# RWKV recurrence in phases: TensorE's order written out between small phases and dense units

## The chip, the core and the metric

The kernel runs on one core of a Trainium2 chip. The metric is the time of one execution in device microseconds; times of several executions are told as a median. TensorE (PE in the rows) does matmuls, and its weight loads are a row of their own (PEld); VectorE is DVE, ScalarE ACT, GpSimd POOL, and SyncE (SP) issues the DMAs. Each engine takes its instructions in the order that was fixed when the kernel was compiled; semaphores between engines make an instruction wait for its operands and buffers.

## The reference

One inference step of a two-layer trunk for 512 prompt tokens and 8 samples of 4 tokens, 1024 features. Layer 0 is a SwiGLU, RWKV-7 time mixing and a second SwiGLU; layer 1 has mLSTM in place of RWKV. All in float32. The change is in layer 0, whose core is the recurrence over tokens, with 16 heads of 64 and a state S (64 x 64) for each head:

```python
def step(S, inp):
    r_t, d_t, k_t, v_t, kk_t, b_t = inp
    sa = jnp.einsum('bhvk,bhk->bhv', S, -kk_t)
    S = S * d_t[:, :, None, :] + sa[..., None] * b_t[:, :, None, :] + v_t[..., None] * k_t[:, :, None, :]
    return S, jnp.einsum('bhvk,bhk->bhv', S, r_t)
```

Ahead of it stand the mixes of neighbouring tokens, the projections r, k, v and the low-rank projections of decay, a and gate; behind it a group norm per head, a bonus term, the gate and the output projection.

## The kernel before

**Dense work.** Weights are streamed from HBM in blocks of 128 x 1024 float32 and split into a high and a low part by ScalarE and VectorE (`weight`, `split`, L352 and L353); `mm3` (L356 to L358) then does three matmuls for each 128 x 128 tile. The tokens are worked on in two parts: part 0 is prompt tokens 0 to 255 (256 columns), part 1 prompt tokens 256 to 511 and the 32 sample tokens (288 columns). A unit of dense work is a closure: 24 matmuls for a projection, 48 for one block of the SwiGLU's gate and up projections, 12 to 24 for a block of its down projection.

**The recurrence** is done in chunks of 64 tokens, four heads (two pairs) at a time: m = 0 to 3 for part 0, m = 4 to 7 for part 1. For each m there are
- `rwkv_prep`, for each pair: the low-rank product of decay and a, exponentials, scan and scaled keys; tile `swa` and PSUM bank `pq` have one buffer each;
- `rwkv_quad`: Gram products (L937), masks (L940), rounding (L949, L951), the products `e` on GpSimd (L955), and then the inverse of a triangular matrix by doubling, in rounds between TensorE and ScalarE or VectorE (L959 to L993);
- `rwkv_tokens`: values transposed, bonus;
- `rwkv_chunk`, four times (c = 0 to 3): three rounds between TensorE and VectorE, which carry the state;
- `rwkv_sample` for part 1, for each pair: the samples' own recurrence. It loads the state into `s0` (one buffer, L1076), multiplies it (L1104), and at the end adds the last product (L1135) to it (L1136) and stores it (L1137);
- `rwkv_finish`: norm, gate and split of the pair's output.

`rwkv_slots` goes through 32 slots, t = 4 m + c. In each it writes the chunk, at c = 0 also the quad and values of m + 1, at c = 2 the preparation of m + 2, and at c = 3 the finishes. All of it stands under `high_priority(OFF)`, which puts it ahead of dense work wherever it can run; the scheduler of the compiler, which plays the program through with its own costs, then fixes the order of each engine. After each slot an equal share of the dense units `todo` is written. Slots 0 to 9 have the rest of the first SwiGLU of part 1 and then norm, mixes and the r and k projections of part 1 (`rwkv_first(1)`), slots 10 to 15 its k, gate and v projections, slots 17 to 31 the output projection of part 0 (`rwkv_out(0)`) and its second SwiGLU; `rwkv_out(1)` follows.

Of the kernel before, what the change touches and what calls it, by code (L numbers as in the profile page):

```python
# [28 lines left out]
OFF = 20000  # L29
NMX = 19  # L30
# [218 lines left out]

class Trunk:  # L250
    def __init__(self, tc, nc, a, o, pool):
        self.tc, self.nc, self.a, self.o, self.pool = tc, nc, a, o, pool
        self.n = 0
        self.last = None
        self.hn = {}
        self.V, self.S, self.G, self.T = nc.vector, nc.scalar, nc.gpsimd, nc.tensor

# [203 lines left out]
    def ffn_units(self, name, g, i, groups=(0, 8, 15, FT)):  # L461
# [18 lines left out]
        def up(m):  # L480
            pg, pu = self.bank("pd", 2), self.bank("pd", 2)
            for ps, n in ((pg, "_g"), (pu, "_u")):
                wt = self.weight(self.a[name + n][m])
                for k in range(KT):
                    c = slice(k * P, (k + 1) * P)
                    self.mm3(ps[:, :w_], *wt(c), xs[k][0], xs[k][1], k == 0, k == KT - 1)
            s, w, e = self.t1(w_), self.t1(w_), self.t1(w_)
            V.tensor_tensor(s, pg[:, :w_], rs, op=ALU.mult)  # L488
            V.tensor_tensor(w, pu[:, :w_], rs, op=ALU.mult)
            self.sigmoid(e, s)  # L490
            G.tensor_tensor(s, s, w, op=ALU.mult)
            G.tensor_tensor(s, s, e, op=ALU.mult)
            h[m] = [self.hm(w_) for _ in range(2)]
            self.split(*h[m], s)

        def down(m, k0, k1):
            wt = self.weight(self.a[name + "_d"][m][:, k0 * P:k1 * P])
            ps = self.bank("pd", 2)
            for k in range(k0, k1):
                c = slice((k - k0) * P, (k - k0 + 1) * P)  # L500
                self.mm3(ps[:, :w_], *wt(c), h[k][0], h[k][1], k == k0, k == k1 - 1)
            V.scalar_tensor_tensor(self.x[m][:, hs], ps[:, :w_], 0.5, self.x[m][:, hs], op0=ALU.mult, op1=ALU.add)
        us = [start]
        for k0, k1 in zip(groups, groups[1:]):
            us += [lambda m=m: up(m) for m in range(k0, k1)]
            us += [lambda m=m, k0=k0, k1=k1: down(m, k0, k1) for m in range(KT)]
# [50 lines left out]
    def rwkv(self, before=None, after=None):  # L557


        with self.scope("rw", nps=1):  # L560
# [4 lines left out]
            with self.tc.tile_pool(name="spill", bufs=1, space=DRAM) as dp:  # L565
# [3 lines left out]
                self.d, self.quad, self.st = {}, {}, {}  # L569
                self.chain, self.chain_y = [self.bank("pc", 2) for _ in range(2)]  # L570
                self.nhm = {"mx": NMX, "hm": 8}
                with self.scope("rw1", nps=0):
# [7 lines left out]
                    with self.tc.high_priority(OFF):  # L580
                        self.rwkv_ahead(0)
                        self.rwkv_square(0)
# [3 lines left out]
                    with self.tc.high_priority(OFF):  # L586
                        self.rwkv_value(0)
                        self.rwkv_ahead(1)
# [6 lines left out]
                with self.scope("rw2", nps=0):  # L595
                    with self.tc.high_priority(OFF):
                        self.rwkv_value(ND)
# [101 lines left out]
    def part_dense(self, w, ps, xs, mw=P, first=True, last=True):  # L699
        for k in range(KT):  # L700
            c = slice(k * mw, (k + 1) * mw)
            self.mm3(ps, *w(c), xs[k][0], xs[k][1], first and k == 0, last and k == KT - 1)

    def rwkv_project(self, n, c, i):
# [12 lines left out]
        return [lambda: xs.extend(self.rwkv_mix(c, i))] + [lambda m=m: unit(m) for m in range(KT)]  # L717

    def rwkv_low_rank(self, i):
# [36 lines left out]
        for c, ns in ((1, (("r_w1", P, slice(0, 64), self.hwa),)), (4, (("r_a1", P, slice(64, P), self.hwa),)),  # L756
                      (5, (("r_g1a", P, slice(0, P), self.hg), ("r_g1b", P, slice(0, 96), None)))):
            us.append(lambda c=c: mix(c))
# [3 lines left out]
    def rwkv_first(self, i):  # L762

        low, k = self.rwkv_low_rank(i), self.rwkv_project("k", 2, i)
        return ([lambda: self.rwkv_norm(i)] + low[:4] + self.rwkv_project("r", 0, i) + k[:5],
# [26 lines left out]
    def rwkv_ahead(self, m):  # L792

        if m < 2 * ND:
            self.d[m] = [self.rwkv_prep(2 * (m % ND) + a, m // ND) for a in range(2)]

    def rwkv_square(self, m):
        if m < 2 * ND:
            self.quad[m] = self.rwkv_quad(self.d[m])

    def rwkv_value(self, m):
        if m < 2 * ND:
            uv = self.rp("uv", 2, [P, 1024]).rearrange("p (a c h v) -> p a c h v", a=2, c=4, h=2)
            for a in range(2):
                self.rwkv_tokens(2 * (m % ND) + a, m // ND, self.d[m][a]["v"], uv[:, a])
            self.quad[m] += (uv,)
# [43 lines left out]
    def rwkv_prep(self, j, i):  # L850
        nc, V, S, G, T = self.nc, self.V, self.S, self.G, self.T
# [10 lines left out]
        for e, rows in enumerate(R):  # L862
            ps = self.bank("pq", 1)[:, :w]
# [12 lines left out]
        S.activation(q, k, AF.Square, scale=self.vec("kk", j))  # L876
        ps = self.bank("pq", 1)[:, :w]
# [29 lines left out]
        return {"xc": xc, "xs": xs, "arc": arc, "ars": ars, "pc": pc, "y": k, "v": v}  # L907

    def rwkv_quad(self, ds):
# [3 lines left out]
        V, S, G, T = self.V, self.S, self.G, self.T  # L913
# [16 lines left out]
        xt = self.rp("xt", 2, [P, 1024])  # L930
# [10 lines left out]

        for a, d in enumerate(ds):
            px = self.bank("pq", 1)
            for i in range(4):
                T.transpose(px[:, i * P:(i + 1) * P], flat(d["xc"][:, i]), self.ident)
            S.copy(xt[:, a * 512:(a + 1) * 512], px)
# [10 lines left out]
        e = part(0)  # L957
        pt = pb()
# [5 lines left out]
        for l in range(1, 6):  # L964
            e = part(l)
            p1 = pb()
            each(lambda r, a, b: T.matmul(p1[r, a], e[r, a], ti[r, a], start=True, stop=True))
            p1s = h16("p1s")
            S.copy(p1s, p1[:, :W])
            pd = pb()  # L970
# [7 lines left out]
        pt = pb()  # L978
        each(lambda r, a, b: T.matmul(pt[r, a], ti[r, a], id16[r], start=True, stop=True))
        S.copy(tt, pt[:, :W])  # L980
        pr = pb()

# [4 lines left out]
        each(residual)  # L987
        r_ = self.rp("e", 2, [P, W], F16)
        V.tensor_tensor(r_, pr[:, :W], ti, op=ALU.subtract)
        pf = pb()  # L990
# [3 lines left out]
        return gm, tf, xt  # L994
# [5 lines left out]
    def rwkv_tokens(self, j, i, v, uv):  # L1000

        V, S, T = self.V, self.S, self.T
        R = (slice(0, 64), slice(64, 128))
        r, k = self.r[i][j], self.k[i][j]
        pv = self.bank("pq", 1)
# [6 lines left out]
        V.scalar_tensor_tensor(r, r, self.vec("rk", j), k, op0=ALU.mult, op1=ALU.mult)  # L1012
        ps = self.bank("pq", 1)[:, :r.shape[-1]]
# [3 lines left out]
    def rwkv_chunk(self, m, c):  # L1017

        V, S, T = self.V, self.S, self.T
        R = (slice(0, 64), slice(64, 128))  # L1020
        gm, tf, xt, uv = self.quad[m]
# [10 lines left out]
        pr, pu, pn = reg(c % 2), reg(2), reg(3)  # L1032
        for a in range(2):
# [5 lines left out]
        V.tensor_copy(rhs, pr)  # L1039
        for a in range(2):  # L1040
# [4 lines left out]
        S.copy(uv[R[0], :, c, 1, :], two(pu[R[0]]))  # L1045
        for a, h in pairs:
            z = (a * 4 + c) * P + h * 64
            T.matmul(pn[R[h], col(a)], xt[:, z:z + 64], uv[:, a, c, h, :], start=True, stop=True)
        sn = self.rp("stp", ND, [P, P]) if m < ND and c == 3 else self.rp("sm", 3, [P, P])
        for a in range(2):  # L1050
            if st is None:
                V.tensor_scalar(sn[:, col(a)], pn[:, col(a)], pc[a], None, op0=ALU.mult)
            else:
                V.scalar_tensor_tensor(sn[:, col(a)], pn[:, col(a)], pc[a], sp[:, col(a)], op0=ALU.mult, op1=ALU.add)
        out = lambda a: slice(a * 4 * CH + c * CH, a * 4 * CH + (c + 1) * CH)
        py = self.chain_y
        for a in range(2):
            for h in range(2):
                T.matmul(py[R[h], out(a)], uv[:, a, c, h, :], gm[:, a, c, 1 - h, 64:128], start=True, stop=st is None)  # L1059
            for h in range(2 if st is not None else 0):  # L1060
                T.matmul(py[R[h], out(a)], st[R[h], col(a)], arc[a][R[h], c, 1, :], start=False, stop=True)
        if c == 3:
# [4 lines left out]
    def rwkv_sample(self, j, d):  # L1067
# [3 lines left out]
        H = slice(0, 64)  # L1071
        xs, ars, y, v, pl = d["xs"], d["ars"], d["y"], d["v"], d["pc"][:, 4:]
# [5 lines left out]
        gm = t5().rearrange("p (h t) -> p h t", h=2)  # L1078
        for h in range(2):
            pg = self.ps()  # L1080
            T.matmul(pg[H, :64], xs[R[h]].rearrange("p x t -> p (x t)"),
                     ars[R[h]].rearrange("p x t -> p (x t)"), start=True, stop=True)
            V.tensor_tensor(gm[H, 1 - h, :], pg[H, :64], self.masks[H], op=ALU.mult)
# [4 lines left out]
                        pl.unsqueeze(1).unsqueeze(3).to_broadcast([P, 2, NB, NS]), op=ALU.mult)  # L1088
        px = self.ps()
        T.transpose(px[H, :P], xs.rearrange("p x t -> p (x t)"), self.ident)  # L1090
        xt = t5()
        S.copy(xt[H], px[H, :P])
        vd = nt[:, 64:128]
        G.tensor_copy(vd.rearrange("p (x t) -> p x t", x=2), v[:, HA:].unsqueeze(1).to_broadcast([P, 2, TS]))
        pv = self.ps()
        T.transpose(pv[H, :P], vd, self.ident)
        uv = t5().rearrange("p (h v) -> p h v", h=2)
        for h in range(2):
            S.copy(uv[Q[h], h, :], pv[Q[h], h * 64:(h + 1) * 64])

        pa = self.ps()
        for b in range(NB):
            for h in range(2):
                T.matmul(pa[R[h], b * 8:(b + 1) * 8], s0v[R[h], b, :],  # L1104
                         ars[R[h], :, b * NS:(b + 1) * NS], start=True, stop=True)
        a0 = t5()
# [491 lines left out]
```

## Time and profile before

| | us |
|---|---|
| median of 3 runs | 2540.12 (2539.03 to 2542.99) |
| profiled execution | 2541.78 |
| its span, first to last instruction | 2539.8 |

| engine | busy us in the span | share |
|---|---|---|
| TensorE matmuls | 2445.1 | 96% |
| TensorE weight loads | 2310.1 | 91% |
| VectorE | 1587.1 | 62% |
| ScalarE | 1250.3 | 49% |
| GpSimd | 501.6 | 20% |

Busy times are sums of instruction times. Matmuls are pipelined, and the ends of the records are modelled, so the distance from start to start tells more than a matmul's own time. Idle time counts gaps longer than 0.15 us. The granted clock is a mean over a stretch, 1.0 being the full 2.4 GHz.

### The profile page before, as it was taken

How to read it: one execution, taken by the hardware profiler on the slowest of the kernel's cores; microseconds unless marked ns; L12 is line 12 of the kernel's file. 1: busy time of each engine (PE TensorE's matmuls, PEld its weight loads, DVE VectorE, ACT ScalarE, POOL GpSimd, SP SyncE). 2: the span in 40 equal slices, each digit the busy share in tenths (PEclk: the TensorE clock that was granted, in tenths of full speed). 3: DMA queues.
4: the chain of work that ended last, by engine and by line, in shares of the span. 5: the costliest groups of instructions: out<-in, count | busy, mean ns of one | idle time of the engine just before them, and what ended most of it. 6: DMA issues, size and time to landing. Idle time of an engine off the chain costs nothing.

```text
span 2539.8 us, 54086 instructions
## 1 busy us (share of the span) xinstructions
PE 2445.1 (96%) x21731; PEld 2310.1 (91%) x21731; DVE 1587.1 (62%) x3154; ACT 1250.3 (49%) x2716; POOL 501.6 (20%) x522
## 2 busy tenths in 40 slices
PE   9998999999889999999999999999999999999997
PEld 8998988888778788897899999999978899999997
DVE  6667787787887886765666544443346856444433
ACT  6555666655575564554555433332245545333322
POOL 1203333333432342322011011110000000111100
PEclk9998999999799899999999999999999999999999
DMA  6664543333233223444455522222223322222222
GB/s 215 183 197 130 166 131 120 105 96 120 90 120 103 75 93 113 129 150 146 128 167 164 153 89 90 84 85 88 83 87 112 101 73 92 86 92 90 88 84 73
DMA packets 102218, 291.62 MB, mean 115 GB/s; under 512 B 12568, under 2 KB 28344, under 8 KB 101968
## 3 DMA queue, kind: packets, MB, share of 16 engines
q1 hardware_dynamic: 101968, 288.18, 36.9%
q8 instruction: 170, 2.79, 0.4%
q14 instruction: 80, 0.66, 0.1%
HBM read 278.76 MB, written 9.38 MB: 113 GB/s over the span
## 4 chain that ended last, share of the span: by engine, by line
PE 84%; DVE 9%; issue 2%; ACT 2%; DMA 1%; POOL 1%; SPq 0%; DVEq 0%; ACTq 0%; POOLq 0%
PE ps L356 17%; PE ps L358 17%; PE ps L357 17%; PE pd L356 7%; PE pd L357 7%; PE pd L358 7%; DVE wl L353 2%; DVE m L693 1%; PE ps L1254 1%; PE ps L1256 1%; PE ps L1255 1%; PE b L937 1%; PE ps L1135 1%; DVE mx L695 1%; PE pc L1059 1%
## 5 line engine op out<-in xcount | busy, mean ns | idle before, releaser
L353 DVE TENSOR_TENSOR wl<-wr,wh 128x512 fp32r<-128x512 f32 (+2 forms) x1025 | 723.2, 708 | 479.6 <-ACT wh L352 452.8
L352 ACT CAST wh<-wr 128x512 fp32r<-128x512 f32 (+2 forms) x1025 | 621.8, 609 | 676.6 <-PE ps L357 430.8
L356 PE MATMUL ps<-a,wh 128*128 128x288 f32 (+1 forms) x2384 | 698.0, 293 | 13.5 <-ACT a L404 5.0
L358 PE MATMUL ps<-a,wl 128*128 128x288 f32 (+1 forms) x2384 | 692.6, 291 | 0.0
L357 PE MATMUL ps<-a,wh 128*128 128x288 f32 (+1 forms) x2384 | 686.6, 288 | 0.3
L356 PEld LDWEIGHTS ps<-a,wh 128*128 128x128 f32 x2384 | 452.8, 190 | 16.9 <-DVE raw L1350 5.4
L357 PEld LDWEIGHTS ps<-a,wh 128*128 128x128 f32 x2384 | 452.6, 190 | 1.5 <-DVE a L405 0.8
L358 PEld LDWEIGHTS ps<-a,wl 128*128 128x128 f32 x2384 | 450.0, 189 | 0.5 <-DVE wl L353 0.2
L428 POOL TENSOR_TENSOR t<-t,t 128x256 f32<-128x256 f32 (+1 forms) x132 | 141.7, 1073 | 846.7 <-ACT wh L352 410.1
L356 PE MATMUL ps<-h,wh 128*128 128x288 f32 (+1 forms) x1056 | 303.9, 288 | 0.0
L357 PE MATMUL ps<-h,wh 128*128 128x288 f32 (+1 forms) x1056 | 303.4, 287 | 0.0
L358 PE MATMUL ps<-h,wl 128*128 128x288 f32 (+1 forms) x1056 | 303.2, 287 | 0.0
L356 PE MATMUL pd<-rk,wh 128*128 128x288 f32 (+1 forms) x656 | 199.0, 304 | 6.8 <-DVE t L488 2.9
L358 PEld LDWEIGHTS ps<-h,wl 128*128 128x128 f32 x1056 | 198.9, 188 | 0.0
L357 PEld LDWEIGHTS ps<-h,wh 128*128 128x128 f32 x1056 | 198.9, 188 | 0.0
L357 PE MATMUL pd<-rk,wh 128*128 128x288 f32 (+1 forms) x656 | 198.6, 303 | 0.2 <-DVE gm L679 0.2
L356 PEld LDWEIGHTS ps<-h,wh 128*128 128x128 f32 x1056 | 198.6, 188 | 0.0
L358 PE MATMUL pd<-rk,wl 128*128 128x288 f32 (+1 forms) x656 | 197.2, 301 | 0.0
L352 ACT CAST h<-t 128x256 fp32r<-128x256 f32 (+1 forms) x132 | 55.3, 419 | 198.9 <-POOL t L428 198.9
L357 PE MATMUL pd<-mx,wh 128*128 128x256 f32 (+1 forms) x448 | 135.3, 303 | 9.4 <-DVE mx L695 6.6
L356 PE MATMUL pd<-mx,wh 128*128 128x256 f32 (+1 forms) x448 | 133.8, 302 | 4.3 <-ACT rk L716 1.9
L356 PEld LDWEIGHTS pd<-rk,wh 128*128 128x128 f32 x656 | 128.0, 195 | 10.5 <-ACT mx L694 2.9
(460 smaller groups left out, 4548.4 us busy)
## 6 DMA issues: line engine op xcount, KB each, us to landing
wr<-in_f0a_u_dram SPq DMA_DIRECT2D x44, 512.0 KB, 3.6
wr<-in_f0b_g_dram SPq DMA_DIRECT2D x44, 512.0 KB, 3.6
wr<-in_f0b_u_dram SPq DMA_DIRECT2D x44, 512.0 KB, 3.5
wr<-in_f0a_g_dram SPq DMA_DIRECT2D x43, 512.0 KB, 3.6
wr<-in_f0b_d_dram SPq DMA_DIRECT2D x24, 512.0 KB, 3.6
wr<-in_f1a_g_dram SPq DMA_DIRECT2D x22, 512.0 KB, 4.6
wr<-in_f1a_u_dram SPq DMA_DIRECT2D x22, 512.0 KB, 3.5
wr<-in_f1b_g_dram SPq DMA_DIRECT2D x22, 512.0 KB, 3.5
```

The lines of the kernel that those rows point to most:

```text
L352: self.S.copy(dst_h, src)
L353: self.V.tensor_tensor(dst_l, src, dst_h, op=ALU.subtract)
L356: self.T.matmul(out, wh, xh, start=start, stop=False)
L357: self.T.matmul(out, wh, xl, start=False, stop=False)
L358: self.T.matmul(out, wl, xh, start=False, stop=stop)
L428: self.G.tensor_tensor(s, s, w, op=ALU.mult)
L693: V.scalar_tensor_tensor(m, d, self.vec("mu", c * 8 + k), xn, op0=ALU.mult, op1=ALU.add)
L695: (self.G if k % 2 else V).tensor_tensor(l, m, h.bitcast(F32), op=ALU.subtract)
L937: T.matmul(pg[:, (1 - h) * 512 + i * P:(1 - h) * 512 + (i + 1) * P], flat(xc[R[h], i]), flat(arc[R[h], i]), start=True, stop=True)
L1059: T.matmul(py[R[h], out(a)], uv[:, a, c, h, :], gm[:, a, c, 1 - h, 64:128], start=True, stop=st is None)
L1135: T.matmul(pn[R[h], :], xt[H, h * 64:(h + 1) * 64], um, start=True, stop=True)
L1254: T.matmul(pss[q][:n, :], xs[k][0][:, ts], wt(cs)[0], start=k == 0, stop=False)
```

## The change

The small work is turned into generators: each function yields "s", "pq" or "ps" ahead of each of its TensorE steps. A slot has `SPS` = 4 steps. A step advances each generator that waits at "s" by one step, then writes a share of the dense work, then advances at most one generator waiting at "pq" and one at "ps" (those that need the single banks of these names), and writes another share. Dense units give their number of matmuls as cost, the SwiGLU's gate and up projections are two units instead of one, and the shares follow cost. `ordered` ties each matmul of a phase, and the first and last of each `mm3`, to the one before, and the matmuls of the phases lose the high priority; the other engines' instructions keep it.

The quad's transposes of the chunk's keys are a generator of their own (`rwkv_rows`). The quad's last transpose goes into the second half of the residual's bank. A chunk's new state is written behind its output products. In the sample's recurrence the state product comes first, two transposes share a bank, and some tiles move from bank `ps` to `pq`; `s0` still has one buffer.

```diff
+class Plain:
+    def put(self, f, a, k):
+        with self.t.tc.high_priority(-self.t.off):
+            return self.t.ordered(f(*a, **k))
...
     def mm3(self, out, wh, wl, xh, xl, start, stop):
-        self.T.matmul(out, wh, xh, start=start, stop=False)
-        self.T.matmul(out, wh, xl, start=False, stop=False)
-        self.T.matmul(out, wl, xh, start=False, stop=stop)
+        T = self.PT if self.off else self.T
+        first = T.matmul(out, wh, xh, start=start, stop=False)
+        T.matmul(out, wh, xl, start=False, stop=False)
+        last = T.matmul(out, wl, xh, start=False, stop=stop)
+        if not self.off and self.in_order:
+            if self.order is not None:
+                self.after(first, self.order)
+            self.order = last
...
+    def ordered(self, r):
+
+        if self.in_order:
+            if self.order is not None:
+                self.after(r, self.order)
+            self.order = r
+        return r
...
+    def rwkv_phase(self, places):
+
+        with self.tc.high_priority(OFF):
+            self.off = OFF
+            seen = set()
+            for name in list(self.gens):
+                place = self.gens[name][1]
+                if place in places and (place == "s" or place not in seen):
+                    seen.add(place)
+                    self.advance(name)
+            self.off = 0
...
+        def dense():
+            nonlocal done, k
+            k += 1
+            while todo and done + todo[0][0] / 2 <= total * k / n:
+                c, f = todo.pop(0)
+                done += c
+                f()
         for t in range(t0, t1):
             m, c = divmod(t, 4)
             i, j = divmod(m, ND)
             with self.tc.high_priority(OFF):
+                self.off = OFF
                 if c == 0:
-                    self.rwkv_square(m + 1)
-
-                    if m + 1 != ND:
-                        self.rwkv_value(m + 1)
+                    self.drain("quad", "px", "value", "ahead", "sample")
+                    if m + 1 < 2 * ND:
+                        self.begin("px", self.rwkv_rows(m + 1))
+                        self.begin("quad", self.rwkv_square(m + 1))
+
+                        if m + 1 != ND:
+                            self.begin("value", self.rwkv_value(m + 1))
+                    if i:
+                        self.begin("sample", self.rwkv_samples(m))
                 if c == 2:
-                    self.rwkv_ahead(m + 2)
-                if i and c in (0, 1):
-                    self.rwkv_sample(2 * j + c, self.d[m][c])
-                self.rwkv_chunk(m, c)
+                    self.begin("ahead", self.rwkv_ahead(m + 2))
+                self.begin("chunk", self.rwkv_chunk(m, c))
+                self.off = 0
+            for q in range(SPS):
+                self.rwkv_phase(("s",))
+                dense()
+                self.rwkv_phase(("pq", "ps"))
+                dense()
+            with self.tc.high_priority(OFF):
+                self.off = OFF
+                self.drain("chunk")
                 if c == 3:
-                    for a in range(2):
-                        self.rwkv_finish(2 * j + a, i, m)
-            self.step(-(-len(self.todo) // (t1 - t)))
+                    self.drain("finish", "sample")
+                    self.begin("finish", self.rwkv_finishes(m))
+                if t == 4 * ND or t == 8 * ND - 1:
+                    self.drain("finish")
+                self.off = 0
...
+        yield "s"
         pr = pb()
+        each(lambda r, a, b: T.matmul(pr[r, b], ti[r, a], id16[r], start=True, stop=True))
...
         each(residual)
+        S.copy(tt, pr[:, W:])
...
         pn = self.ps()
         for h in range(2):
+            yield "s"
             um = self.local("um", 1, [64, 512])
```

## Rows read from the trace of the kernel before

**Rows 1.** Busy time by stretch: stretch, length, engines (instructions), granted clock, DMA share, GB/s.

```profile
core 0: us, PE busy (x) PEld busy (x) DVE busy (x) ACT busy (x) POOL busy (x), PEclk, DMA share, GB/s
404.00:640.00 236.00, 230.87 (x2936) 207.37 (x2935) 185.62 (x380) 145.09 (x338) 75.95 (x73) 0.99 0.37 111
640.00:800.00 160.00, 137.39 (x1136) 122.55 (x1137) 136.38 (x272) 103.12 (x258) 57.28 (x75) 0.86 0.30 93
800.00:1090.00 290.00, 280.19 (x3588) 239.62 (x3587) 211.95 (x450) 157.86 (x377) 97.55 (x98) 0.96 0.34 105
1090.00:1195.00 105.00, 104.83 (x896) 95.37 (x896) 67.13 (x141) 55.95 (x120) 28.94 (x31) 1.00 0.54 164
1195.00:1237.00 42.00, 33.11 (x186) 27.28 (x184) 23.22 (x47) 20.64 (x43) 1.03 (x1) 0.84 0.28 88
```

**Rows 2.** Timeline of TensorE, small groups among dense matmuls: start, duration, line, tiles.

```profile
457.35 0.29 PE L358 MATMUL pd<-hm,wl 128*128 128x288 f32 x1
457.58 0.44 PE L971 MATMUL b<-p1s,ti 64*64 64x64 f16 x16
...
459.13 0.40 PE L356 MATMUL pd<-hm,wh 128*128 128x288 f32 x1
459.37 0.29 PE L357 MATMUL pd<-hm,wh 128*128 128x288 f32 x1
459.50 0.30 PE L358 MATMUL pd<-hm,wl 128*128 128x288 f32 x1
...
1100.30 0.28 PE L356 MATMUL pd<-hm,wh 128*128 128x256 f32 x1
1100.42 0.28 PE L357 MATMUL pd<-hm,wh 128*128 128x256 f32 x1
```

**Rows 3.** Timeline of TensorE: first and last small group of the stretch.

```profile
406.92 0.44 PE L971 MATMUL b<-p1s,ti 64*64 64x64 f16 x16
...
1212.09 0.29 PE L1168 MATMUL ps<-a 96*128 96x288 f32 x1
```

**Rows 4.** Timeline, one quad from its second Gram product to GpSimd's first products.

```profile
996.08 0.93 PE L937 MATMUL b<-a 64*128 64x128 f32 x10
...
997.92 1.29 DVE L940 TENSOR_TENSOR gm<-b,c_c_rw 128x512 f32<-128x512 f32 x2 [0.36 <-PE b L937]
...
1002.80 2.60 POOL L955 TENSOR_TENSOR e<-nh,em 128x512 f16<-128x512 f16 x2
```

**Rows 5.** Timeline, one pair's preparation: second low-rank product, last scaled key.

```profile
536.12 0.38 PE L356 MATMUL pq<-a,lah 64*128 64x256 f32 x1
...
548.96 0.42 DVE L904 TENSOR_TENSOR a<-rk,swa 64x256 f32<-64x256 f32 x1
```

**Rows 6.** Timeline, end of one sample pair and the next load; then L1076's landing.

```profile
1003.79 1.07 PE L1135 MATMUL ps<-um,sa 64*64 64x512 f32 x2
1004.89 0.69 DVE L1136 TENSOR_TENSOR s<-s,ps 128x512 f32<-128x512 f32 x1 [1.42 <-PE ps L1135]
1005.61 0.34 SPq L1137 DMA_DIRECT2D out_sS_dram<-s  x1
1007.66 0.33 SPq L1076 DMA_DIRECT2D s<-in_S_dram  x1
...
DMA to landing us min/median/max: 2.6/3.4/3.8
```

**Rows 7.** Timeline, normalisation of part 1: last input, first shift, first mix's end.

```profile
638.58 0.45 DVE L502 SCALAR_TENSOR_TENSOR x<-pd,x 128x288 f32<-128x288 f32 x1
...
643.36 0.82 POOL L674 TENSOR_TENSOR hm<-x 128x255 f32<-128x255 f32 x1 [19.30 <-DVE x L658]
...
659.22 0.91 POOL L695 TENSOR_TENSOR mx<-m,mx 128x288 fp32r<-128x288 f32 x1 [0.86 <-ACT mx L694]
```

**Rows 8.** Timeline of TensorE at the tail: first finish, output's wait for the second.

```profile
1200.59 0.82 PE L1151 MATMUL ps<-rk,c_c_rw 128*128 128x288 f32 x2 [0.78 <-DVE s L1136]
...
1214.72 0.81 PE L356 MATMUL pd<-rk,wh 128*128 128x288 f32 x2 [2.34 <-ACT rk L352]
```

More of the change, by code (lines that the diff above doesn't have):

```diff
@@ L29 @@
 OFF = 20000
+SPS = 4
 NMX = 19
@@ L247, in __getitem__, with __init__, __call__, matmul @@
         return self.d[k + self.by]
+class Unit:
+    def __init__(self, *parts):
+        self.parts = parts
+    def __call__(self):
+        for _, f in self.parts:
+            f()
+class Plain:
+    def __init__(self, t, engine):
+        self.t, self.engine = t, engine
+    def matmul(self, *a, **k):
+        return self.put(self.engine.matmul, a, k)
+    def transpose(self, *a, **k):
+        return self.put(self.engine.transpose, a, k)
+    def put(self, f, a, k):
+        with self.t.tc.high_priority(-self.t.off):
+            return self.t.ordered(f(*a, **k))
 class Trunk:
@@ L480, in up, with half, second @@
         def up(m):
[L481 to L494, printed above, removed]
+            ps = []
+            def half(n):
+                ps.append(self.bank("pd", 2)[:, :w_])
+                self.part_dense(self.weight(self.a[name + n][m]), ps[-1], xs)
+            def second():
+                half("_u")
+                s, w, e = self.t1(w_), self.t1(w_), self.t1(w_)
+                V.tensor_tensor(s, ps[0], rs, op=ALU.mult)
+                V.tensor_tensor(w, ps[1], rs, op=ALU.mult)
+                self.sigmoid(e, s)
+                G.tensor_tensor(s, s, w, op=ALU.mult)
+                G.tensor_tensor(s, s, e, op=ALU.mult)
+                h[m] = [self.hm(w_) for _ in range(2)]
+                self.split(*h[m], s)
+            return Unit((24, lambda: half("_g")), (24, second))
         def down(m, k0, k1):
@@ L794, in rwkv_ahead @@
         if m < 2 * ND:
-            self.d[m] = [self.rwkv_prep(2 * (m % ND) + a, m // ND) for a in range(2)]
+            self.d[m] = []
+            for a in range(2):
+                yield from self.rwkv_prep(2 * (m % ND) + a, m // ND, self.d[m])
     def rwkv_square(self, m):
         if m < 2 * ND:
-            self.quad[m] = self.rwkv_quad(self.d[m])
+            yield from self.rwkv_quad(m, self.d[m])
     def rwkv_value(self, m):
@@ L804, in rwkv_value, with rwkv_samples, rwkv_finishes, begin @@
             for a in range(2):
[L805 to L808 removed]
+                yield from self.rwkv_tokens(2 * (m % ND) + a, m // ND, self.d[m][a]["v"], uv[:, a])
+            self.uv[m] = uv
+    def rwkv_samples(self, m):
+        i, j = divmod(m, ND)
+        for a in range(2):
+            yield from self.rwkv_sample(2 * j + a, self.d[m][a])
+    def rwkv_finishes(self, m):
+        i, j = divmod(m, ND)
+        for a in range(2):
+            yield from self.rwkv_finish(2 * j + a, i, m)
+    def begin(self, name, gen):
+        self.gens[name] = [gen, next(gen, None)]
+    def advance(self, name):
+        g = self.gens[name]
+        g[1] = next(g[0], None)
+        if g[1] is None:
+            del self.gens[name]
+    def drain(self, *names):
+        for name in names:
+            while name in self.gens:
+                self.advance(name)
[7 more added lines that the diff above has]
+                    seen.add(place)
+                    self.advance(name)
+            self.off = 0
+    def rwkv_slots(self, t0, t1):
+        todo = [p for u in self.todo for p in (u.parts if isinstance(u, Unit) else ((24, u),))]
+        self.todo = []
+        total, left, n = sum(c for c, _ in todo), 0, 2 * SPS * (t1 - t0)
+        done, k = 0, 0
+        self.in_order = True
+        def dense():
[4 more added lines that the diff above has]
+                done += c
+                f()
         for t in range(t0, t1):
@@ L993, in rwkv_quad, with rwkv_rows @@
         V.tensor_tensor(tf, tt, pf[:, :W], op=ALU.add)
-        return gm, tf, xt
+        self.quad[m] = gm, tf, self.xt[m]
+    def rwkv_rows(self, m):
+        self.xt[m] = xt = self.rp("xt", 2, [P, 1024])
+        for a, d in enumerate(self.d[m]):
+            yield "pq"
+            px = self.bank("pq", 1)
+            for i in range(4):
+                self.PT.transpose(px[:, i * P:(i + 1) * P], d["xc"][:, i].rearrange("p x t -> p (x t)"), self.ident)
+            self.S.copy(xt[:, a * 512:(a + 1) * 512], px)
     def wide_bank(self):
```

138 lines of the change are left out of this document (80 added, 58 removed).

## Prediction

> **What bounds the kernel now.** I read the share of each engine first, then a table of stages, then single stretches of the timeline. Nearly all of the change lies between 404 us, where the recurrence's slots begin, and 1237 us, where the mixer's output is done: 833 us. In this stretch TensorE is busy for 786.4 us, the sum of the five stages, and idle for 46.6: 5.1 at 404 to 640, 22.6 at 640 to 800, 9.8, 0.2 and 8.9 [rows 1]. VectorE, the next engine, is busy for 624 us, 79% even in the stage in which the chain runs fastest [rows 1]. So TensorE's stream of work is the bound, and what can be won is idle time, time at the low clock, and time lost in switching.
>
> The granted clock of the stages (0.99, 0.86, 0.96, 1.00, 0.84) gives the time at the lower level, 1.2 GHz against 2.4: twice the missing share, 5 + 45 + 23 + 0 + 13 = 86 us [rows 1]. Idle time inside it costs nothing more, so the clock costs between (86 - 42) / 2 = 22 and 43 us; I take 30. What remains is **work: 833 - 47 - 30 = 756 us**.
>
> **What a switch costs.** The dense matmuls follow each other at 0.13 us (288 columns) and 0.12 us (256). The last one ahead of a small group takes 0.23 us to the next start instead of 0.13, and the first one behind a group takes 0.24 [rows 2]. So a small group costs about 0.10 + 0.11, say 0.19 us with the 256-column units, beside its own work. The timeline of the stretch has 238 such groups; the first and the last are in [rows 3].
>
> **What the change does to TensorE's work.** Counted in the code, 1152 dense matmuls fall into slots 0 to 9, 336 into slots 10 to 15, none into slot 16, 1776 into slots 17 to 31; 269 stand before the slots and 192 behind. No matmul is taken away but for a few in the quad (its last transpose goes into the bank of the residual, which saves one round through ScalarE). A slot has four steps, and each step an "s" phase, a dense share, a "pq"/"ps" phase and another share. All 128 "s" phases have work; of the other 128 phases about 58 have. Where a dense share is smaller than half a unit it is empty, and neighbouring phases merge. I count 165 groups instead of 238: 73 x 0.19 = 14 us less. **Work after: 742 us**.
>
> From this the length of a step follows. Dense shares: 28.8 matmuls x 0.13 = 3.7 us in slots 0 to 9, 14 x 0.13 = 1.8 in slots 10 to 15, 29.6 x 0.12 = 3.6 in slots 17 to 31. All dense work in slots is 150 + 44 + 213 = 407 us; 742 - 407 - 35 before - 25 behind leaves 275 us of small work and switches, 2.15 us for each of 128 steps. A step lasts 5.9, 4.0, 2.1 (slot 16) and 5.7 us. Whatever must happen between two steps of one generator has this time; if it takes longer, TensorE stands still, and behind the waiting matmul stand the dense unit that was ready, the other generators' steps, and with them ScalarE's and VectorE's weight splits, whose buffers the dense unit would free. In the kernel before, a ready dense unit takes such a place.
>
> **The waits, term by term.**
> - Quad, from the second Gram product to the first transpose: masks on VectorE, rounding on ScalarE, two subtractions and a product on GpSimd. The product issued at 1002.80 is the first of two in 2.60 us and ends at 1004.1, so 8.0 us after the Gram matmuls began at 996.08; from the mask's start at 997.92 it is 6.2 [rows 4]. One step is given, 5.9 or 5.7, so a wait of 0.3 to 2.1; I take 1.2. Three quads in slots 0 to 11, two in 20 to 27: 5 x 1.2; one in slots 12 to 15: 4 (slot 16 has its own term). 10 us; bounds 2 and 18.
> - Preparation of a pair: the second low-rank product began at 536.12 and the last scaled key ended at 549.38, 13.3 us [rows 5]. `swa` and the bank `pq` are single, so the second matmul of the pair's other half, two steps later, can't be written before the first half is done. Two steps are 11.8, 8 and 11.4 us: 2 x 2 + 2 x 5.8 + 2 x 2.4 = 20 us with this row, 0 if queueing on VectorE made half of it. I take 10.
> - Sample state: its tile `s0` is single. The last product began at 1003.79, the add at 1004.89, the store at 1005.61, the next load at 1007.66, and a load lands 3.4 us after its issue: 7.3 us in all, and the next pair's state product needs it [rows 6]. Before, this stood beside dense work. Now it is in the order: each pair takes 9 "s" steps, a slot group has 16 for two pairs, so two steps are drained at the end of the fourth slot and the next pair follows at once, with some 2.4 us of TensorE work from that product's start on (its own pair took 1.07, the next quad's first Gram product and the value transposes the rest, an estimate): 3 x 4.9. Inside a group one step of 5.7 stands between: 4 x 1.6. 21 us; bounds 8 and 30.
> - Slot 16 has no dense work at all. Its four steps wait for the state's load (3.4), for the quad's 8.0 us (less one step of 2.1), and about 2 us each for two evacuations: 13 us; bounds 6 and 20.
> - Normalisation of the second half: its last input was written at 638.58, GpSimd began the shifts at 643.36 and ended the first mix at 660.13, 21.5 us [rows 7]. Behind the first projection all phases now wait. Two phases (2 us) and the projection's own matmuls (3.2) cover it: 16 us. The kernel before has this wait too, in its 22.6 us of idle at 640 to 800.
> - The tail: the last two finishes and the output's second unit run one behind the other from 1200.59 to 1214.72 [rows 8]. Nothing dense is left in either kernel: 12 us, as now.
> - All other phases: the quad's inner steps, the chunk's and the finishes' fit in 5.7 us when the mask's 1.3 us of VectorE [rows 4] is the longest evacuation, less well in 4.0. 8 us; bounds 0 and 64 (0.5 us at each of 128).
>
> Sum 10 + 10 + 21 + 13 + 16 + 12 + 8 = **90 us of idle instead of 47**. The clock: the same ratio to idle as now (30 to 47) would give 57, but half of these waits are long ones at few places, each with one recovery; I take 32, bounds 20 and 57.
>
> Stretch after: 742 + 90 + 32 = 864 us against 833: +31. The profiled execution took 2541.78 us (span 2539.8), 1.7 above the median of the three runs; 2541.8 + 31 = 2572.8, as a median 2571. **Forecast 2571 us**, own range 2548 to 2600.
>
> **Rivals.**
> - *Written order hides its waits (faster).* Chains need a step or less: quad and preparation wait 0, the samples 12 (stores and loads start early), slot 16 takes 8, and norm 16 and tail 10 stay: 46 us idle, clock 20. 742 + 66 = 808, -25: 2515 us. For it: at 404 to 640 the chain ran fast with 5.1 us idle and VectorE at 79% [rows 1]; after the change chain work is spread more evenly. Against it: 21.5, 13.3, 8.0 and 7.3 us [rows 4 to 7] are all longer than the step. It decides if these waits fall under some 60 us in sum. Gains end near 2490: norm, tail and slot 16 stay.
> - *Each phase is late.* VectorE, at 79% already, answers 0.5 us late at each of 128 phases: 64 instead of 8 us and 13 us more of clock, +100: 2640 us. For it: the same engine splits all weights; against it: two units of weights are split ahead.
> - *The clock falls at every wait.* The stage with 22.6 us of idle in 160 had 0.86, that with 5.1 in 236 had 0.99 [rows 1]; if the waits, spread as they are, hold the whole stretch at 0.86, it has 2 x 0.14 x 864 = 242 us at the low level, less 90 idle, half of it: 76 us instead of 32, +75: 2615 us. Against it: the stage at 800 to 1090 has waits too and 0.96 [rows 1]. The Trainium skill ("TensorE: Matmul & The Clock Gate", section HAM oscillation) states this mechanism: waits between bursts of matmuls drop the engine to half rate, again at each burst. By that rule this rival, by the rows of most stages the forecast.
> - *The order doesn't matter.* The earlier order was a fixed list too, and waits move rather than grow: within 5 us.
>
> **How the numbers follow.** Forecast 0.46, faster rival 0.30, late phases 0.10, clock 0.06, no difference 0.08. A measurement of this kernel can tell about 0.2% (5 us) from no change; faster 0.30, same 0.08, slower 0.62. The range 2510 to 2630 leaves out most of the late phases and the end of the faster case. Cases of both signs weigh much; the forecast's own range is above.
>
> **What would show it.** Right: idle before the state product at three group borders of about 5 us, before the quad's first transpose of 1 to 2, a nearly empty TensorE in slot 16, and dense runs of 24 unbroken matmuls between groups; TensorE idle of some 90 us in the stretch. Wrong: idle under 60 us with a clock above 0.95, or the slots starting much before 447 us (404 + 35 dense + 8 small), or the chain's pace under 5.7 us a step.

## The result, and the profile after

| | us |
|---|---|
| before, median of 4 runs on the same chip | 2539.57 (2538.57 to 2542.99) |
| after, median of 4 runs | 2621.98 (2620.36 to 2623.67) |
| ratio | 1.0322 [1.0308, 1.0336] |

The kernel became 82 us slower; 31 were forecast. The time lies inside the wide range of 2510 to 2630 but outside the forecast's own range of 2548 to 2600, and the size is wrong by more than a factor of two. The page of the changed kernel (span, engines; TensorE's busy share and granted clock in 40 slices of the span):

```profile
span 2618.4 us, 54036 instructions
PE 2452.8 (94%) x21731; PEld 2322.9 (89%) x21731; DVE 1590.2 (61%) x3154; ACT 1255.5 (48%) x2716; POOL 495.6 (19%) x522
PE   9998999895978889988899999999999999999997
PEclk9998999897889889898899999999999999999998
```

TensorE is busy for nearly as long as before and has as many matmuls; busy share and clock are lower than before in slices 8 to 20. There the recurrence's slots lie. Up to 404 us the two kernels agree, and behind the mixer's output within 4 us: the stretch of 833 us now ends at 1319 instead of 1237, so the 82 us are in it. The stages of [rows 1], now cut at the starts of slots 0, 10, 16 and 17, at the end of slot 31 and at the output's end (stretch, length, engines, granted clock, DMA share, GB/s):

```profile
404.00:440.00 36.00, 35.14 (x357) 32.47 (x355) 29.12 (x55) 24.82 (x56) 9.70 (x10) 1.00 0.41 122
440.00:726.00 286.00, 243.20 (x2658) 221.22 (x2657) 210.35 (x400) 156.75 (x365) 93.37 (x111) 0.89 0.34 102
726.00:850.00 124.00, 97.53 (x1277) 84.24 (x1276) 91.74 (x197) 69.44 (x169) 26.44 (x27) 0.89 0.23 72
850.00:875.00 25.00, 18.98 (x189) 13.68 (x190) 11.46 (x25) 10.83 (x28) 7.87 (x8) 0.71 0.04 13
875.00:1277.00 402.00, 363.85 (x4038) 321.43 (x4037) 260.64 (x564) 203.35 (x470) 113.99 (x121) 0.91 0.37 112
1277.00:1319.00 42.00, 35.61 (x211) 31.44 (x210) 24.07 (x48) 21.42 (x44) 1.08 (x1) 0.84 0.33 105
404.00:1319.00 915.00, 794.31 (x8723) 704.48 (x8721) 627.38 (x1284) 486.61 (x1132) 252.45 (x277) 0.90 0.33 101
```

TensorE is idle for 915 - 794.3 = 121 us instead of 47, and the granted clock is 0.90 instead of 0.95 over the stretch. VectorE is busy for 627 us, where it was 624. What ended TensorE's waits in this stretch (engine, tile, line, releaser: us in total, times, longest):

```profile
PE pd L387 <- ACT hm L382: 19.0, 5, 5.6
PE ps L274 <- DMA s<-in_S_dram: 16.8, 7, 4.3
PE pq L274 <- ACT swa L833: 13.7, 9, 4.0
PE pd L387 <- ACT mx L732: 11.1, 2, 6.2
PE pd L388 <- POOL mx L733: 9.0, 5, 5.3
PE b L274 <- POOL e L1073: 6.5, 4, 3.2
```

In the kernel before, the largest entry of the same view is 3.7 us; these two were the longest there:

```profile
PE pc L1042 <- DVE sm L1039: 3.7, 2, 3.2
PE pq L356 <- ACT swa L787: 3.6, 2, 2.7
```

Five of the six are in the forecast: the samples' state (16.8, forecast 21), the preparation (13.7, forecast 10), the mixes of part 1 (20.1 in two lines; the forecast had 16 for the normalisation with the first mix) and the quad's `e` (6.5, forecast 10). The largest is not. One instance of it in TensorE's timeline (start, duration, line, tiles; in brackets the idle time ahead and who ended it):

```profile
490.93 0.29 PE L389 MATMUL pd<-rk,wl 128*128 128x288 f32 x1
491.06 0.59 PE L274 MATMUL pq<-a,c_c_rw 128*128 128x256 f32 x2
491.30 0.48 PE L387 MATMUL pd<-hm,wh 128*128 128x288 f32 x1
...
492.55 0.29 PE L389 MATMUL pd<-hm,wl 128*128 128x288 f32 x1
498.17 0.61 PE L387 MATMUL pd<-hm,wh 128*128 128x288 f32 x1 [5.32 <-ACT hm L382]
```

The last up projection of a group of SwiGLU blocks (`rk` is its operand) ends at 491; then one phase; then the first down projection. After nine matmuls it stands for 5.3 us for the tile `hm` that has to be made from that last up projection. All that follows, phases too, is written behind it. Written order makes dense work wait for dense work too. The wait on the samples' state has the other form (same view):

```profile
900.94 0.22 PE L274 MATMUL ps<-ars,xs__1970_10423 64*64 64x64 f32 x1
903.67 1.10 PE L274 MATMUL ps<-ars,s 64*64 64x8 f32 x32 [2.51 <-DMA s<-in_S_dram]
904.70 0.69 PE L274 MATMUL pq<-a,lah 64*128 64x288 f32 x2
...
906.77 0.41 PE L389 MATMUL pd<-rk,wl 128*128 128x256 f32 x1
906.98 0.41 PE L387 MATMUL pd<-rk,wh 128*128 128x256 f32 x1
```

Here a phase waits for the load, and the dense unit behind it stands with it (its operand `rk` had been in use up to 900.4). And the matmuls of that unit then follow each other at 0.21 us instead of the 0.12 of [rows 2]: the clock has fallen to its lower level, and the granted clock of 904 to 908 us is 0.61. Each of the 24 stretches at the lower level between 404 and 1319 us comes behind one or more waits; the least is a single one of 0.7 us.

The wait at 903.67 stands inside a group of slots, between its two pairs. At the border of two groups the next quad stands between (same view, another stretch):

```profile
951.83 1.15 PE L274 MATMUL ps<-um,sa 64*64 64x512 f32 x2 [1.21 <-POOL um L1278]
952.91 2.08 PE L274 MATMUL b<-a 64*128 64x128 f32 x16
...
958.47 0.93 PE L274 MATMUL ps<-ars,s 64*64 64x8 f32 x26 [1.27 <-DMA s<-in_S_dram]
```

**Where the 82 us are.** From the starts of TensorE's records I split the stretch, for this kernel and for those of the experiments, into idle time; the clock's cost (in the stretches at the lower level, what a dense matmul takes above the 0.13 or 0.12 us of [rows 2], and half the time of small matmuls); and the rest, which is work with its switches. Idle time by the starts is up to 3 us more than length less busy time. Groups are runs of small matmuls between dense ones, counted alike for all kernels (234 for the kernel before, where the prediction's count has 238).

| kernel | median us | stretch | groups | idle | at the low clock | clock's cost | work |
|---|---|---|---|---|---|---|---|
| before | 2539.6 | 833 | 234 | 47 | 85 | 35 | 751 |
| after | 2622.0 | 915 | 147 | 122 | 191 | 74 | 719 |
| no order (e1_free) | 2552.8 | 840 | 289 | 36 | 51 | 21 | 783 |
| no order, high priority (e2_free_high) | 2527.9 | 828 | 224 | 46 | 92 | 37 | 745 |
| only phases ordered (e10_dense_free) | 2550.0 | 842 | 194 | 62 | 137 | 55 | 725 |
| two `s0` (e3_two_s0) | 2594.6 | 889 | 146 | 108 | 171 | 64 | 717 |
| up ahead of down (e4_lag) | 2611.2 | 902 | 149 | 113 | 188 | 70 | 718 |
| both (e6_s0_lag) | 2575.1 | 866 | 148 | 97 | 130 | 50 | 719 |
| six steps (e8_sps6) | 2668.9 | 966 | 144 | 154 | 229 | 89 | 723 |

So +82 = idle 75 + clock 39 - work 32. The forecast had +31 = idle 43 + clock 2 - work 14.

### The profile page after: what moved, and what is told of

The parts are those of the page before. It is cut to its first block, busy times and chain, and to the rows that moved or that the text cites. A ratio compares the mean times of both kernels' runs of the same rounds, so it can differ in the third digit from the quotient of the medians.

```text
span 2618.4 us, 54036 instructions
## 1 busy us (share of the span) xinstructions
PE 2452.8 (94%) x21731; PEld 2322.9 (89%) x21731; DVE 1590.2 (61%) x3154; ACT 1255.5 (48%) x2716; POOL 495.6 (19%) x522
## 4 chain that ended last, share of the span: by engine, by line
PE 82%; DVE 9%; ACT 3%; DMA 3%; issue 2%; POOL 1%; SPq 0%; DVEq 0%; ACTq 0%; POOLq 0%
PE ps L387 17%; PE ps L389 17%; PE ps L388 16%; PE pd L387 7%; PE pd L388 7%; PE pd L389 6%; PE ps L274 2%; PE b L274 2%; PE pc L274 2%; DVE wl L383 2%; PE pq L274 2%; DVE m L731 1%; DMA s<-in_S_dram 1%; PE ps L1402 1%; PE ps L1404 1%
## 5 line engine op out<-in xcount | busy, mean ns | idle before, releaser
L383 DVE TENSOR_TENSOR wl<-wr,wh 128x512 fp32r<-128x512 f32 (+2 forms) x1025 | 731.2, 715 | 519.6 <-ACT wh L382 497.8
L387 PE MATMUL pd<-mx,wh 128*128 128x256 f32 (+1 forms) x448 | 139.2, 311 | 14.2 <-ACT mx L732 12.4
L388 PE MATMUL pd<-mx,wh 128*128 128x256 f32 (+1 forms) x448 | 137.3, 307 | 15.1 <-POOL mx L733 9.0
```

Of the source, the lines that this page charges most:

```text
L383: self.V.tensor_tensor(dst_l, src, dst_h, op=ALU.subtract)
L387: first = T.matmul(out, wh, xh, start=start, stop=False)
```

## Experiments

**Is it the order at all?** The order is taken away, and nothing else:

```diff
         if not self.off and self.in_order:
-            if self.order is not None:
-                self.after(first, self.order)
-            self.order = last
...
         if self.in_order:
-            if self.order is not None:
-                self.after(r, self.order)
-            self.order = r
```

> The changed kernel without its written order: the dependencies that tie each matmul of a phase and each dense matmul to the one before are taken away, all else stays (the generators, the shares, the quad's shorter ending). Theory: the written order makes the waits, since a ready dense unit may not pass a waiting phase. Then TensorE's gaps in the stretch from 404 us to the end of the mixer fall from 122 us to 50 to 60, the time at the low clock from 191 to about 90 us, and the time goes to about 2545 us. Rival: the even spread of the chain's steps makes them, or the longer chain of the phases; then the time stays above 2590 us.

Measured: 2552.8 us (2546.8 to 2555.7), 69 less than after; ratio to before 1.0058 [1.0037, 1.0079]. Idle 36 us, less even than before, and 51 us at the low clock; both fell further than expected. What it loses to the kernel before is work, 783 instead of 751 us, with 289 groups instead of 234. In the next one the phases' matmuls also keep the high priority:

```diff
 class Plain:
     def put(self, f, a, k):
-        with self.t.tc.high_priority(-self.t.off):
-            return self.t.ordered(f(*a, **k))
+        return f(*a, **k)
```

> As the kernel without the order, but the phases' matmuls keep the high priority too, as in the kernel before. Theory (the written order makes the waits): about 2540 us, the time of the kernel before, or a few us less by the quad's saved round. Rival (the spread in steps itself costs): over 2580 us. If this one is fast and the kernel without order but at plain priority is not, the loss comes from the place that the scheduler gives the phases' matmuls and not from the ties.

Measured: 2527.9 us (2523.6 to 2532.8), ratio 0.9953 [0.9939, 0.9968]: 94 us less than after, and a little faster than the kernel before. The generators, the shares by cost and the quad's shorter ending therefore cost nothing; the loss comes with the order. Two things came with it: taking the ties away gives 69 us, and giving the phases' matmuls their high priority back another 25.

**Which part of the order?** Only the first half of the first diff is made, so the phases stay tied to each other, but dense matmuls may pass them.

> The changed kernel with only the dense matmuls set free: the matmuls of the phases stay tied to each other in their written order and at plain priority, but the first and last of a dense product are no longer tied to the ones before. Theory (the loss comes because a ready dense unit may not pass a waiting phase): about as fast as the kernel without any order, 2553 us, so 2545 to 2560. Rival (the order of the small phases among each other holds them up, since one late chain stops the other chains): over 2590 us.

Measured: 2550.0 us (2546.7 to 2553.4), ratio 1.0049 [1.0030, 1.0067]. The stretch (columns as above):

```profile
404.00:1246.00 842.00, 780.66 (x8691) 685.51 (x8690) 628.32 (x1283) 482.42 (x1131) 258.36 (x277) 0.92 0.36 109
```

Idle 61 us instead of 121. The state's load and ScalarE's `hm` are no longer among the waits, ScalarE's `mx` has 0.6; the one on `swa` still has 8.6. So 72 of the 94 us hang on the ties of the dense matmuls: the chains are late in this kernel too, but a ready dense unit fills the time. The ties of the phases among each other cost nothing that can be seen (2550.0 with them, 2552.8 without); what is left of the 94 us comes with the phases' plain priority.

**The wait on the samples' state.** The edit, without the line that makes the `hm` tiles narrower:

```diff
-        s0 = self.local("s0", 1, [P, 512])
+        s0 = self.local("s0", 2, [P, 512])
```

> The changed kernel with two buffers for the samples' state s0 instead of one (the rounded SwiGLU tiles hm get narrower by the unused columns to make room). Theory: the six waits of the state product on the load of s0, 16.8 us in the trace, are the store, the load and the landing behind each other, and each wait costs clock as well: 2605 to 2598 us, 17 us less by the wait and 0 to 7 by the clock. Rival: the wait is only the first of several at the group's border (evacuation of the sample's last product, the next quad) and something else is late in its place: within 5 us of 2622.

Measured: 2594.6 us (2593.1 to 2605.7), ratio 1.0228 [1.0202, 1.0255], 27 less than after. The line of the load is gone from the waits; the next two hardly change:

```profile
PE pd L387 <- ACT hm L382: 18.9, 5, 5.6
PE pq L274 <- ACT swa L833: 14.5, 10, 4.0
```

Idle falls by 14, the clock's cost by 10. The same edit was made in the kernel before and in the one without order:

> The kernel before with two buffers for s0. Theory (its wait stands beside dense work, and shows at most at the tail, where the last pair's load follows the store of the pair before): 2533 to 2541 us, a gain of 0 to 6 us. Rival (the wait costs there as it does after the change): about 2515 us.

Measured: 2539.3 us (2536.8 to 2544.9), ratio 1.0004 [0.9994, 1.0015]: nothing.

> The kernel without the order and with the phases' matmuls at high priority (2528 us), with two buffers for s0 as well. Theory (without the order dense work stands in the place of the wait on s0): a gain of 0 to 5 us only, 2523 to 2528 us, where the same edit gave 27 us under the written order. Rival (the chain of the samples ends late anyway and sets the tail of the stretch): 2510 to 2520 us.

Measured: 2536.6 us (2532.3 to 2548.2), ratio 0.9997 [0.9984, 1.0010]: no gain, even 9 us more than without the edit. I take it that the scheduler, which plays the program through anew after each edit, chose otherwise elsewhere; no run shows it. The 12 us that e2_free_high is faster than before are of the same size, and I don't explain them. The trace of e2_free_high has 2.2 us of waits on this load, that of the kernel before none that ends so. So the single `s0` costs 27 us under the written order, and no gain from a second one shows without it.

**The wait of dense work on dense work.** The first gate and up unit of the next group is written ahead of a group's down projections. The limits of the groups change with it (not shown; in part 0, 7, 7 and 8 blocks instead of 8, 7 and 7):

```diff
-            us += [up(m) for m in range(k0, k1)]
+            us += [up(m) for m in range(k0 + (k0 > lag), min(k1 + (k1 > lag), FT))]
```

> The changed kernel with another order of units in the SwiGLU: the first gate and up unit of the next group of blocks is written ahead of a group's down projections (in part 1 three groups of 4, one of 3, 3 and the rest; in part 0 the groups stay). Theory: the down projection waits 19.0 us in sum for the last tile hm of its group, because nothing may stand between under the written order; 24 dense matmuls, 3 us, in between take away 12 to 15 us of idle time and 3 to 8 us at the low clock: about 2602 us. Rival: the wait goes to the next unit (the weight split is what is late): 2615 to 2625 us.

Measured: 2611.2 us (2608.4 to 2612.5), ratio 1.0283 [1.0266, 1.0300], 11 less: between the two. The waits show why:

```profile
PE ps L274 <- DMA s<-in_S_dram: 20.5, 7, 4.6
PE pq L274 <- ACT swa L833: 17.0, 11, 4.0
...
PE pd L387 <- ACT hm L382: 5.0, 2, 2.9
```

`hm` lost 14 us, but the chain, which had caught up during these waits, is waited for 7 us more at `s0` and `swa`. Then both edits together:

> The changed kernel with both edits: two buffers for s0, and the first gate and up unit of the next group written ahead of a group's down projections. Alone they gave 27.4 and 10.8 us. Theory: two separate waits, each with its own share of clock, so the gains add up: 2584 us. Rival: waits move on to the next late thing under the written order (in the run with the other order of units the waits on s0 grew from 16.8 to 20.5 us); then the two together give more than the sum, since this growth is taken away too, about 2578 us, or less than the sum, over 2590 us, if something third (mixes, preparation) is late at the same places.

Measured: 2575.1 us (2573.6 to 2580.3), ratio 1.0146 [1.0131, 1.0161]: 47 less than after, more than 27 + 11. Idle 97, clock 50. The rival held: the two give 9 us more than their sum. That part of one edit's gain had gone into the wait that the other removes fits the numbers; the growth at `s0` was 3.7 us, and the rest would be clock.

**The length of a step.** `SPS` 6 instead of 4.

> The changed kernel with six steps to a slot instead of four, so a step lasts some 4.8 us instead of 7.2 in slots 0 to 9. Theory (under the written order a phase waits for what its chain needs above the length of a step): more of the inner waits show, the preparation's and the quad's e by 2 us each at some 12 places, the samples and mixes as now, and more small groups: 2645 to 2690 us. Rival (the waits are set by the borders of slots and the dense units' own waits): within 10 us of 2622.

Measured: 2668.9 us (2665.6 to 2672.9), ratio 1.0513 [1.0494, 1.0532]. The chain's inner waits grow, `swa` from 13.7 to 24.7 and `e` from 6.5 to 14.4, and those on `hm` and on the state's load don't; the groups didn't grow in number as expected (144, after 147):

```profile
PE pq L274 <- ACT swa L833: 24.7, 13, 7.3
PE pd L387 <- ACT hm L382: 15.2, 5, 4.5
PE b L274 <- POOL e L1073: 14.4, 7, 4.6
PE ps L274 <- DMA s<-in_S_dram: 12.7, 5, 4.4
```

For these inner waits it is as the prediction reckoned: a wait is what a chain needs above its steps.

**What a wait costs in clock.** Into the dense first SwiGLU of layer 1, where the changed kernel has a clock of 1.00 and no idle time, 21 waits are put (or 21 bursts of small matmuls; what these compute is not used). The matmuls of this SwiGLU are tied in their written order in all three kernels; with the bursts TensorE is idle for 1 us in the whole stretch, so the ties alone bring no wait there. `N` is 5 or 1:

```diff
+                if name == "f1a" and m and i == 0:
+                    z = self.local("z", 1, [P, 256])
+                    self.S.copy(z, prev[:, :256])
+                    for _ in range(N):
+                        self.G.tensor_scalar(z, z, 0.5, None, op0=ALU.mult)
+                    self.ordered(self.T.matmul(pg[:, :8], self.ones, z[:, :8], start=True, stop=True))
```

> The changed kernel with a wait of TensorE put 21 times into the dense first SwiGLU of layer 1, where the granted clock is 1.0 and TensorE stands still nowhere: ahead of each gate and up unit but the first, one tiny matmul waits for a copy of the previous unit's bank by ScalarE and five operations of GpSimd on 128x256, by estimate some 3.5 us. Theory (a wait of a few us lowers the clock, and dense work behind it pays): each wait costs its idle time and 1.5 to 2.5 us more, a growth of 105 to 125 us, with a low stretch of 4 us or more behind most of the 21 waits. Rival (idle time costs only itself, the clock falls for the small work): the growth is the idle time, some 75 us, and the clock stays above 0.97 there outside the idle time.

> The same with one operation of GpSimd instead of five, a wait of 1 to 1.8 us, 21 times. Theory (the clock's price comes with longer waits only): the growth is the idle time, 21 to 38 us, and no or few low stretches. Rival (each wait that can be seen costs clock): 30 us or more above the idle time.

> The changed kernel with a burst of 128 small matmuls (64x64 float32, no wait) put 21 times into the same dense SwiGLU. One costs 0.05 to 0.09 us by the small products in the trace, so a burst 6 to 12 us and all 130 to 250 us. Theory (a stretch of small matmuls alone lowers the clock, as at 904.9, 959.5, 1133.6 and 1239.4 us in the trace of the changed kernel): low stretches in or behind most of the 21 bursts, clock of the stage under 0.92. Rival (only idle time does): clock 1.0, no low stretch.

Measured: 2813.9 (2807.1 to 2819.5), 2727.4 (2722.8 to 2729.4) and 2788.3 us (2782.7 to 2791.5), ratios 1.1081 [1.1060, 1.1102], 1.0739 [1.0721, 1.0757] and 1.0979 [1.0963, 1.0996]. The waits of the first (its first wait was longer than the others, which took 6.5 us):

```profile
PE ps L459 <- POOL z L458: 142.4, 21, 12.4
```

And those of the second, 2.8 us each but for the first:

```profile
PE ps L459 <- POOL z L458: 64.1, 21, 8.7
```

The stretch that holds the 21 places, in the kernel with long waits (columns as above):

```profile
1541.00:1976.00 435.00, 292.58 (x1982) 287.64 (x1982) 113.51 (x207) 94.64 (x189) 129.94 (x147) 0.82 0.17 51
```

In the one with short waits:

```profile
1546.00:1889.00 343.00, 278.92 (x1967) 273.97 (x1967) 113.47 (x207) 94.33 (x188) 57.67 (x63) 0.90 0.21 64
```

And in the one with bursts of small matmuls:

```profile
1540.00:1990.00 450.00, 448.99 (x7633) 443.64 (x7632) 127.49 (x233) 99.68 (x191) 43.10 (x44) 1.00 0.19 57
```

The waits were about twice as long as I had estimated. The growth over the changed kernel is 191.9 and 105.4 us; less the idle time that leaves 49.5 and 41.3, which is **2.4 us for each wait of 6.5 us and 2.0 for each of 2.8** (the tiny matmul and its switches are in it). The clock alone, reckoned from the stretches at the lower level as in the table, cost 2.1 and 1.5 us for each wait. The clock fell after all 21 long waits and 18 of the 21 short ones. So a wait of less than half the length costs 0.7 times as much clock: the price goes more by the number of waits than by their length. My expectation for the short ones (idle time alone) was wrong. The Trainium skill ("TensorE: Matmul & The Clock Gate", section HAM oscillation) describes this: waits between bursts drop the engine to half rate again at each burst; these two runs agree. The waits in the Trainium skill's example are longer, some 3 to 5 us; here 2.8 us were enough in 17 of 20 cases. The 21 bursts of small matmuls without a wait took 7.9 us each (166.3 / 21) and left the clock at 1.00, against my expectation of less than 0.92: these bursts don't lower it, the waits do. A mix of small work and many short waits may do it too: e10_dense_free has 62 us of idle and 55 of clock's cost, the highest ratio in the table. No run separates that.

## Why the prediction was wrong in size

- **Direction and cause: right.** It said that idle time is what the written order adds, since a ready dense unit may not stand in for a waiting phase. e1_free and e10_dense_free show it: 69 and 72 us go with the ties. The prediction has no term for the phases' lost priority, which makes up some 25 us between e1_free and e2_free_high.
- **The failing step: the clock at 32 us.** "The same ratio to idle as now (30 to 47) would give 57, but half of these waits are long ones at few places, each with one recovery; I take 32." That correction was the error. The cost is 74 us after and 35 before. The ratio to idle is 0.61 after and 0.52 to 0.62 in the other kernels with the whole written order, near the 0.64 that the prediction had worked out and put aside. Had it stayed, 90 us of idle would have brought 57, and the sum 2596 instead of 2571; the rest of the clock's miss comes with the larger idle time. The picture behind it was wrong as well: the waits did not become few and long. TensorE has 40 waits of 1 us or more in the stretch where it had 21, and the clock's cost for each is 74 / 40 = 1.9 us after and 35 / 21 = 1.7 before, beside the 1.5 and 2.1 of the 21 waits put in. This is 37 of the 51 us missing.
- **The idle term: 122 instead of 90.** The missing entry is the SwiGLU's down projection behind its last up projection, 19 us ("all other phases" had 8 in all). The list asked of the chain's phases how long each waits, and not of the dense units; but under a written order these wait too. The normalisation and its mixes took 21 us at 629 to 668 us, forecast 16, and the later mixes another 9; `swa` 13.7 instead of 10 (the 20 us in that term are 17 by its own rows: 2 x 1.5 + 2 x 5.3 + 2 x 1.9). Too high were the quad (6.5, forecast 10), slot 16 (25 - 19 = 6 idle, forecast 13) and the tail: "12 us, as now" is 8.9 in [rows 1], and 6 came. The idle term makes +32 of the 51 in all.
- **The samples' wait came near by luck.** In sum it is 16.8 us, forecast 21. But the waits at the three borders of groups were 1.3, 1.1 and 4.3 us, where 4.9 each was forecast: at the first border the pair's last product and the next quad took 5.4 us (951.83 to 957.2), where 2.4 was reckoned. Inside the groups the waits were 2.5, 1.7, 3.3 and 2.6 us, forecast 1.6.
- **The work: -32 instead of -14.** There are 87 groups fewer instead of 73, and each saved 0.37 us instead of 0.19. The dense side alone is 0.19, as in [rows 2] (45.1 us above the bare pitch before, 28.9 after); the first and last small matmuls of a group lose 0.15 as well, which I didn't count. The price isn't the same everywhere: e1_free has 55 groups more than the kernel before and 32 us more work, 0.58 for each. -18 of the 51: this error hid a part of the other two.
- **The steps.** Slots started at 440 (forecast 447). A step took 7.15, 5.2 and 6.7 us in the three parts, where 5.9, 4.0 and 5.7 were forecast: longer by the waits themselves and by the clock. Dense runs of 24 were unbroken, as said. The sign "about 5 us at three group borders" failed at two of them. TensorE wasn't nearly empty in slot 16 but 19 of 25 us busy.
- **The rivals.** "The clock falls at every wait" put the clock at 76 us and the time at 2615, nearest to what came, with a chance of 0.06. Its mechanism is the one that the 21 waits show; what spoke against it, the clock of 0.96 at 800 to 1090 [rows 1], was a stage with only 6 waits of 1 us or more, and the clock fell 4 times in it. "Each phase is late" fails: VectorE's instructions for the phases (`sb`, `rk`, `ti` and smaller ones) end 14 us of waits, not 64. "Written order hides its waits" fails at its own condition, waits under some 60 us.

## What to carry to other kernels

Before an order is written out by hand, list the waits of everything in it, dense units too: each that an overtaking unit covered until now comes into the open, and edits then help only one by one, since the next late thing takes part of each gain. In this kernel a wait of TensorE of 1 us or more cost its length and some 2 us of clock; in another, count the waits and take the price from its own rows. If small work is to be grouped, tie the small matmuls to each other and leave the dense ones free: of the 94 us, 72 hung on that. Grouping won nothing here even so: e10_dense_free, with 194 groups, is 0.5% slower than the kernel before.

## What was not expected of the hardware

- A wait of 2.8 us in dense work costs nearly as much beyond its idle time as one of 6.5: 2.0 and 2.4 us, of which 1.5 and 2.1 are clock.
- Bursts of 64x64 products alone, 7.9 us each and without a wait, leave the granted clock at 1.00.
- A switch from dense to small matmuls and back costs 0.37 us in all between the kernels before and after: 0.19 at the dense matmuls on both sides, the rest within the small group.
